# A hybrid attention and state-space layer on one core: the p product moved ahead of the output product, more halves turned through memory, more low parts made by transfer

## The chip, the cores and the metric

The kernel runs on 1 core of one Trainium2 chip. Times are device microseconds of one execution, and the median of several executions stands for a kernel. Besides them there is a profile of one execution: it records when each instruction of each engine ran. PE is the tensor engine (matmuls), PEld its weight loads, DVE the vector engine, ACT the scalar engine, POOL the GpSimd engine, SP the sync engine, which only issues transfers.

## What is computed

One layer on 256 tokens of width 1024, batch 1, everything in float32:

```
h = RMSNorm(x);  [q|k|v|z|xBC|dt|g_a|g_b] = h @ W_in                    # 1024 -> 10272
y_a = attention(q, k, v) @ W_o_attn                                     # 16 heads of 64, causal
y_b = mamba2(z, xBC, dt) @ W_o_ssm                                      # 32 heads of 64, 4 groups, state 128
x = x + (sigmoid(g_a) * y_a + sigmoid(g_b) * y_b) @ W_out
x = x + SwiGLU(RMSNorm(x))                                              # D_FF 2816
x = x + (p @ W_ple_proj) * sigmoid(RMSNorm(x) @ W_ple_gate)             # p: 256 wide
```

With 256 tokens the block attention is plain causal attention, computed in two query tiles of 128.

## The kernel before

**Numbers in three products.** Every operand of a large matmul is split into a rounded high part and a low part (`wh`, `wl` for weights), and a product is made of three matmuls, high by high, high by low and low by high. A weight tile is 128 partitions by 2 x 512 (512 KB). SP loads it into one of 4 buffers `raw`, ACT writes the rounded copy `wh`, DVE subtracts and writes `wl` (`split_w`, line 377). For the tile numbers listed in `BY_DMA` DVE is left out: ACT writes the negated rounded copy into `wl`, and a transfer issued by POOL adds the weights from memory onto it (line 399); then ACT writes `wh`. Tiles are numbered in the order of use from the third panel on, four to a panel of 512 columns.

**Panels.** `PANELS` is the order in which PE goes through the mixers' products: column panels of `W_in` (kinds q, k, v, z, xbc, and the gates ga and gb), then those of `W_o_ssm` (yb, group 0 to 3) and of `W_o_attn` (ya), each for two halves n = 0 and 1 of 512 output columns. A panel of kind xbc is either made by rows, in which the weights are the stationary operand and the result comes out transposed, or by tokens. The list `WIDE` names the xbc and z panels by rows that use the wide form: one matmul of 512 columns, `wh` against both parts of the tokens side by side, and one of 256, `wl` against the high part; ACT copies one half of the result out and DVE adds the other (line 1392). The narrow form has three matmuls of 256 columns, and its result is read where it lies.

**Fillers.** The small work (attention, the scan, the splitting of activations) is written as generators. A counter `fill.now` counts the tensor engine's estimated time, and a generator is taken up when the counter has passed its due time; the tables `LAG` hold those delays, `FLIP` the order inside a few groups of products. A scheduler then sets the order on each engine by rank ("hot", "w", "ev", "bg"), and `follow` adds an order between two instructions.

**Transposes.** They are made in two ways. On PE: a matmul against `ident` (line 297), four of 128x128 for a pair of tiles in `split_pair`. Through memory: DVE transposes blocks of 32 (`turn`, line 739), a transfer writes them to a buffer `turn_d` ("put", lines 749 and 770), and four transfers read them back in the other order ("get", line 759). `MOVED_P` names the pairs of heads whose attention probabilities go through memory (six PE transposes each otherwise). In the class `Sent` the table `VIA` names the engines whose queues issue put and get: p for POOL, s for SP, a for ACT. A name in `FIRST` asks that at most three more low parts (line 377) are made on DVE ahead of the block transposes.

**From the mixers to the feed-forward part.** `joined(n)` makes the gated sum m of half n, and its splitted transpose is the stationary operand of the output product (`pair(m_act, ...)`). That product is made of four pieces: first half of m into result halves n = 0 and 1, then second half of m into n = 0 and 1, 24 matmuls of 512 columns each. `res2.take(n)` adds x, which gives r, and r is split and transposed for the gate and up products. Before the change the first half of m goes through memory and the second is transposed on PE (8 transposes) in the first half of the output product; r's first half goes through memory and its second half is transposed on PE (8 transposes) during the p product (`p @ W_ple_proj`, 24 matmuls), which stands between the output product and the gate product. The gate product begins with r's second half (order of k: 4, 6, 0, 2). After the down product both halves of the next sum, e, go through memory. The p product's result is used only at the very end.

Of the kernel before, what the change touches and what calls it, by code (L numbers as in the profile page):

```python
# [48 lines left out]
    ('k', 1, 1536),  # L49
    ('yb', 0, None),  # L50
    ('z', 2, 4096),
    ('xbc', 3, 6656),
    ('yb', 1, None),
    ('v', 1, 2560),
    ('ga', 1, 8736),
    ('ga', 0, 8224),
    ('yb', 2, 0),
    ('yb', 3, 0),
    ('ya', 0, None),
# [9 lines left out]
def by_rows():  # L69
# [4 lines left out]
WIDE = [('xbc', 0), ('xbc', 2), ('xbc', 3), ('xbc', 4), ('xbc', 5), ('z', 1), ('z', 3)]  # L74
# [15 lines left out]
    "dt": [7695],  # L90
    "dt.t": [1912],
    "dt.e": [44376],
    "dt.low": [0],
    "dt.end": [3600],
    "c.get": [6048, 20580, 4500, 8000, 13800, 5850],
    "z.get": [11120, 4880, 4500, 13235],
    "x.get": [11000, 20471, 9085, 6932],
    "qk.get": [11305, 10811, 11000, 4500],
    "c.moved": [13200, 28401, 10992, 18427, 8500, 31353],
    "c.rows": [0, 1200, 570, 3578, 5000, 1374],  # L100
    "x.moved": [11861, 8500, 57827, 23735],
    "x.start": [4956, 3240, 11800, 11000],
    "x.end": [13264, 5000, 2000, 770],
    "p.moved": [13735, 13200, 13600, 8500, 9650, 8500, 16654, 8500],
    "qk.moved": [10248, 13200, 8500, 8500],
    "qk.split": [0, 3450, 5180, 0],
    "xbc.end": [2853, 15120, 2049, 6195, 16486, 27735],
    "z.turn": [0, 2545, 3366, 0],
    "z.moved": [21550, 8500, 10000, 12100],
    "z.end": [0, 6300, 0, 10600],  # L110
    "qk": [32916, 1650, 4275, 500],
    "qk.turn": [36000, 14411, 4575, 1286],
    "qk.t": [24405, 10000, 1000, 2988, 12758, 5403, 0, 2100],
    "qk.end": [1243, 4652, 5346, 500],
    "v": [500, 8545],
    "cb": [6988, 300, 3282, 0],
    "rows": [32],
    "prep": [590, 750, 3484, 10000, 6191, 5565, 4616, 500],
    "seg": [1326, 0, 2000, 1800, 0, 2818, 0, 810, 0, 0, 4892, 630, 6248, 1305, 0, 0],
    "seg.next": [13744, 2000, 11459, 9286, 0, 13729, 13051],  # L120
    "out": [3000, 14599, 3000, 5070],
    "out.xdt": [300, 10600, 0, 4300],
    "out.end": [0, 1696, 0, 4100],
    "off": [3476, 6856, 3829, 437],
    "off.end": [300, 4316, 925, 2950],
    "finish": [10772, 12064, 10000, 0],
    "finish.ones": [5961, 3915, 3675, 13859],
    "sc": [6504, 10000, 5930, 0, 6130, 2000, 5000, 10000],
    "sc.tr": [2000, 10000, 3000, 13779, 0, 13854, 12691, 0],
    "tr": [0, 14560, 28603, 7222, 8494, 500, 5002, 0],  # L130
    "tr.val": [12661, 0, 3856, 2000],
    "val.end": [7236],
    "m": [11900, 6200],
    "res": [5337, 5987],
    "m.moved": [11625, 22875],
    "r.moved": [15000],
# [53 lines left out]
def tile_layer(ctx: ExitStack, tc: tile.TileContext, head, xk, pt, vec, w_dt, w_big, w_dn2, w_pp, out):  # L190
# [995 lines left out]
    def split_pair(toks, jj, cols, rank="bg"):  # L1186
# [3 lines left out]
        with prio(rank):  # L1190
            pm = pb([2, T])
            for tt in range(2):
                for j in range(2):
                    transpose(pm[:, j, tt * P : tt * P + P], toks[tt][:, (2 * jj + j) * P : (2 * jj + j) * P + P], rank == "hot")
            if cols is None:
                o, ol = both[:, :, 0], both[:, :, 1]
                act(o, pm)
                nc.vector.tensor_sub(ol, pm, o.bitcast(F32))
            else:
                for j in range(2):  # L1200
                    rounded = act(both[:, j, 0], pm[:, j], scale=cols[2 * jj + j])
                for j in range(2):
                    last = stt(both[:, j, 1], pm[:, j], cols[2 * jj + j], both[:, j, 0].bitcast(F32), op0=ALU.mult, op1=ALU.subtract)
                fill.split = last.ins
                fill.rounded = rounded.ins
# [39 lines left out]
    def joined(n, ps=None):  # L1245

        acc, ga = accs[n], gates["ga", n]
        sent = Sent("m") if n == 0 else None
        with prio("ev"):
            for tt in range(2):  # L1250
# [3 lines left out]
                if sent:  # L1254
                    sent.send(tt, acc[:, tt])
        toks = [acc[:, 0], acc[:, 1]]
        if sent:
# [161 lines left out]
    class Residual:  # L1419
# [7 lines left out]
        def take(self, n, pan):  # L1427
            b = self.base[n]
            sent = Sent("r" if self.normed else "e") if self.normed == (n == 0) else None
            with prio("hot"):  # L1430
                for tt in range(2):
                    nc.vector.tensor_add(b[:, tt], pan.ps[tt], b[:, tt])  # L1432
                    if sent:
                        sent.send(tt, b[:, tt])
            if not self.normed:
                if n == 0:
                    fill.spawn(split_moved([b[:, 0], b[:, 1]], self.cols(n), self.acts[n], lag("res") + 20000.0), 0)
                elif sent:
                    fill.spawn(split_moved([b[:, 0], b[:, 1]], self.cols(n), self.acts[n], lag("res"), sent), 0)
                else:  # L1440
                    fill.spawn(split_t([b[:, 0], b[:, 1]], self.cols(n), self.acts[n], lag("res")), 0)
            elif n == 0:
                fill.spawn(split_moved([b[:, 0], b[:, 1]], self.cols(n), self.acts[n], lag_of("r.moved", 0), sent), 0)
# [30 lines left out]
    pair(m_act, res2.take, both=True)  # L1474


    pj = [s4([2, 512]) for _ in range(2)]
    ready = [(1, 0), (1, 1)]
    for n in range(2):
        pan = Panel()  # L1480
        parts = load(w_pp[n], 2)
        for tt, pc in enumerate(pan.pieces):
            for k in range(2):
                pan.step(pc, parts[k], (p_h[:, k], p_l[:, k]), k == 1)
                if 4 * n + 2 * tt + k in SPLITS:
                    res2.split(*ready.pop(0))
        with prio("ev"):
            for tt in range(2):
                copy = nc.vector.tensor_copy(pj[n][:, tt], pan.ps[tt])
                if n == 1:  # L1490

                    follow(copy.ins, fill.split)

# [178 lines left out]
```

## Time and profile before

| what | value |
|---|---|
| median of 3 runs | 574.41 us (574.36 to 575.73) |
| the profiled execution: time | 575.04 us |
| its span, first to last instruction | 573.3 us |
| granted clock of PE | 1.000 |
| PE busy | 567.6 us, 99% |
| PE weight loads | 476.0 us, 83% |
| DVE busy | 443.6 us, 77% |
| ACT busy | 339.2 us, 59% |
| POOL busy | 110.4 us, 19% |
| bytes moved | 124.11 MB, 216 GB/s |

The profiled execution took 0.63 us more than the median, and 1.74 us of its time lie outside the span. Matmuls are pipelined: the mean of one matmul in a group is its duration from start to end, and the next may start long before that end. What a matmul costs PE is the distance from its start to the next start.

### The profile page before, as it was taken

What the parts mean: (1) busy time and instruction counts of PE and PEld (TensorE: products, weight loads), DVE (VectorE), ACT (ScalarE), POOL (GpSimd) and SP (SyncE); (2) the same over time, 40 slices, a digit from 0 to 9 for tenths busy, and PEclk for the clock granted to TensorE, in tenths of its full rate; (3) what the DMA queues carried; (4) which work ended last, traced back from release to release, by engine and by line L of the source; (5) the groups of instructions that cost most, each with busy time, mean ns of one, the idle gap of its engine ahead of it and who ended that gap; (6) DMA issues with size and microseconds to landing.
All of it is one profiled execution on the core that took longest, in us unless ns stands there. A gap on an engine that the chain in (4) does not pass through costs nothing.

```text
span 573.3 us, 8490 instructions
## 1 busy us (share of the span) xinstructions
PE 567.6 (99%) x2971; PEld 476.0 (83%) x2971; DVE 443.6 (77%) x702; ACT 339.2 (59%) x532; POOL 110.4 (19%) x163
## 2 busy tenths in 40 slices
PE   9999999999999999999999999999999999999996
PEld 8887898988888888888887888888888888888885
DVE  6678899989999988898695977766767767646564
ACT  6855567676769578748574444645455455444452
POOL 2011223000532413211320200300312112202020
PEclk9999999999999999999999999999999999999999
DMA  9885698656476756758655786585887887857752
GB/s 314 326 259 179 220 264 234 208 159 181 156 189 183 205 176 174 255 166 252 188 168 186 248 275 225 168 274 183 259 287 228 237 255 246 255 177 254 221 149 74
DMA packets 41179, 124.11 MB, mean 216 GB/s; under 512 B 5424, under 2 KB 10576, under 8 KB 41136
## 3 DMA queue, kind: packets, MB, share of 16 engines
q1 hardware_dynamic: 34432, 104.82, 57.1%
q0 software_dynamic: 6128, 18.09, 12.3%
q10 hardware_dynamic: 576, 0.66, 0.4%
q8 instruction: 23, 0.38, 0.3%
q14 instruction: 20, 0.16, 0.1%
HBM read 114.16 MB, written 9.32 MB: 215 GB/s over the span
## 4 chain that ended last, share of the span: by engine, by line
PE 95%; DVE 2%; DMA 1%; issue 1%; ACT 0%; ACTq 0%
PE g L275 84%; PE pb L275 8%; PE pb L297 2%; DMA raw<-in_w_big 1%; PE pb L309 1%; DVE s L653 1%; DVE wl L377 0%; ACT wh L254 0%; DVE s L660 0%; DVE s L1392 0%; ACT s L254 0%; DVE s L1585 0%; DVE s L1586 0%; DVE tiny_dt L600 0%; DVE tiny_dt L609 0%
## 5 line engine op out<-in xcount | busy, mean ns | idle before, releaser
L275 PE MATMUL g<-wh,s 128*128 128x512 f32 (+1 forms) x1220 | 382.0, 390 | 0.0
L254 ACT ACTIVATE wh<-raw 128x1024 fp32r<-128x1024 f32 (+2 forms) x192 | 198.7, 1039 | 165.1 <-PE g L275 128.9
L377 DVE TENSOR_TENSOR wl<-raw,wh 128x1024 fp32r<-128x1024 f32 (+2 forms) x188 | 223.7, 1194 | 85.4 <-ACT wh L254 83.7
L275 PEld LDWEIGHTS g<-wh,s 128*128 128x128 f32 x1220 | 228.7, 189 | 47.7 <-issue 0.5
L275 PE MATMUL g<-wl,s 128*128 128x512 f32 (+1 forms) x610 | 235.7, 388 | 0.0
L275 PEld LDWEIGHTS g<-wl,s 128*128 128x128 f32 x610 | 114.6, 188 | 23.0 <-issue 0.4
L275 PE MATMUL g<-s,wh 128*128 128x512 f32 (+1 forms) x320 | 90.3, 353 | 0.2 <-DVE s L1392 0.2
L275 PE MATMUL g<-s,wl 128*128 128x256 f32 x256 | 69.2, 283 | 0.0
L275 PEld LDWEIGHTS g<-s,wh 128*128 128x128 f32 x320 | 54.8, 190 | 7.2 <-DVE s L1392 0.6
L275 PEld LDWEIGHTS g<-s,wl 128*128 128x128 f32 x256 | 48.5, 189 | 2.0 <-issue 0.2
L749 POOL DMA_DIRECT2D turn_d<-s x28 | 21.7, 775 | 140.5 <-DVE s L739 140.5
L759 POOL DMA_DIRECT2D s<-turn_d x64 | 35.4, 570 | 57.4 <-DMA turn_d<-s 41.4
L254 ACT ACTIVATE s<-s 128x512 f32<-128x512 f32 (+4 forms) x45 | 34.8, 785 | 16.2 <-DVE s L1432 5.6
L275 PEld LDWEIGHTS pb<-s,s 128*64 128x64 f32 (+2 forms) x336 | 23.9, 158 | 5.8 <-issue 2.4
L275 PE MATMUL pb<-s,s 128*64 128x128 f32 (+5 forms) x336 | 28.7, 294 | 0.0
L254 ACT ACTIVATE s<-pb 128x512 f32<-128x512 f32 (+3 forms) x45 | 20.3, 480 | 13.7 <-PE pb L275 8.4
L254 ACT ACTIVATE s<-s,vecs 128x256 f32<-128x256 f32 (+1 forms) x48 | 23.3, 536 | 5.6 <-DMA s<-turn_d 4.6
L653 DVE SCALAR_TENSOR_TENSOR s<-s,vecs,s 128x255 f32<-128x255 f32 (+2 forms) x60 | 26.5, 480 | 0.0
L886 POOL TENSOR_SCALAR_AFFINE_SELECT rr<-a_h 128x512 fp32r<-128x512 f32 x16 | 16.6, 1094 | 38.7 <-PE pb L275 22.4
L739 DVE STREAM_TRANSPOSE s<-s 128x512 f32<-128x512 f32 (+2 forms) x34 | 22.0, 660 | 1.8 <-ACT s L254 1.5
L254 ACT ACTIVATE s<-s,tiny 128x128 f32<-128x128 f32 (+1 forms) x44 | 18.7, 444 | 5.9 <-DVE tiny L1086 5.9
L794 POOL TENSOR_TENSOR tiny<-tiny,mhalf 128x8 f32<-128x8 f32 x8 | 13.2, 1647 | 42.3 <-DVE tiny L792 42.3
(152 smaller groups left out, 379.9 us busy)
## 6 DMA issues: line engine op xcount, KB each, us to landing
raw<-in_w_big SPq DMA_DIRECT2D x176, 512.0 KB
turn_d<-s POOLq DMA_DIRECT2D x24, 256.0 KB, 5.0
s<-turn_d POOLq DMA_DIRECT2D x48, 128.0 KB, 5.3
wl<-in_w_big POOLq DMA_DIRECT2D x5, 512.0 KB, 8.2
raw<-in_head SPq DMA_DIRECT2D x4, 512.0 KB
s<-in_xk SPq DMA_DIRECT2D x4, 512.0 KB
raw<-in_head SPq DMA_DIRECT2D x6, 256.0 KB
turn_d<-s POOLq DMA_DIRECT2D x6, 192.0 KB, 3.1
```

What stands on the lines that cost most here:

```text
L254: return nc.scalar.activation(o, i, f, **kw)
L275: ins = nc.tensor.matmul(o, lhsT, rhs, start=start, stop=stop).ins
L297: queue(nc.tensor.transpose(o, i, ident[: i.shape[0], : i.shape[0]]).ins, main)
L309: nc.tensor.matmul(pw[:, :P], zero, zero, start=True, stop=True)
L377: low = nc.vector.tensor_sub(wl, raw, wh.bitcast(F32))
L653: stt(cc[j][:, sft:], pu[:, j, : T - sft], cw[j][3 - sft], cc[j][:, sft:], op0=ALU.mult, op1=ALU.add)
L739: turned_by.append(nc.vector.transpose(t_.rearrange("p b (x j) -> p x b j", j=32), src.rearrange(f"p {dims[1]} -> p x b j", b=4, j=32)).ins)
L749: nc.gpsimd.dma_start(d[:, :, at : at + t_.shape[2]].rearrange("b p n -> p b n"), t_)
L759: by[via[b % len(via)]].dma_start(o[32 * b : 32 * b + 32], d[b].rearrange("(a i) n -> i a n", i=32))
L794: nc.gpsimd.tensor_tensor(f, ms, mhalf, op=ALU.pow)
L886: nc.gpsimd.affine_select(r, bcast(a_h[:, c, h0 : h0 + 4].bitcast(F32), P), pattern=[[0, 4], [1, P]], compare_op=ALU.is_ge, fill=0.0, base ...
```

## The change

1. **The p product stands ahead of the output product** and takes its own accumulators (`Panel(aside=True)`); p is loaded and split three panels before the end of `PANELS` (`load_p`).
2. **Both second halves there go through memory**: m's second half (`m1`) and r's second half (`r`), put by SP and read by ACT's queue (`VIA` "s", "a"). r's first half is now the one that PE transposes, inside the last piece of the output product, and the gate product takes k in the order 0, 2, 4, 6.
3. **A fourth pair of probabilities**, (1, 0), goes through memory.
4. **More low parts by transfer**: `BY_DMA` has 11 tiles instead of 5.
5. Panel xbc 1 takes the wide form. `WIDE` loses z 3, which is made by tokens before and after, so that the entry had no effect.
6. z 2 is one place earlier and v 1 two places; of the last panels ya 0 and the first half of yb 3 change places. Nearly all numbers of `LAG` and `FLIP` are new.

```diff
-WIDE = [('xbc', 0), ('xbc', 2), ('xbc', 3), ('xbc', 4), ('xbc', 5), ('z', 1), ('z', 3)]
+WIDE = [('xbc', 0), ('xbc', 1), ('xbc', 2), ('xbc', 3), ('xbc', 4), ('xbc', 5), ('z', 1)]
...
-    ('yb', 3, 0),
-    ('ya', 0, None),
+    ('ya', 0, None),
+    ('yb', 3, 0),
...
-    "res": [5337, 5987],
-    "m.moved": [11625, 22875],
-    "r.moved": [15000],
+    "e.moved": [23750],
+    "r.t": [2062],
+    "m.moved": [19988, 8500],
+    "r.moved": [8500],
...
-MOVED_P = {(1, 1), (1, 2), (1, 3)}
-BY_DMA = {25, 37, 46, 53, 63}
-FIRST = ("e",)
-VIA = {"m": ("p", "p"), "r": ("p", "p"), "e": ("s", "sa")}
-SPLITS = (4, 6)
+MOVED_P = {(1, 0), (1, 1), (1, 2), (1, 3)}
+BY_DMA = {22, 24, 26, 37, 45, 46, 48, 52, 58, 66, 75}
+FIRST = ("m1", "r", "e")
+VIA = {"m0": ("p", "p"), "m1": ("s", "a"), "r": ("s", "a"), "e": ("s", "sa")}
...
-            parts = split_pair(toks, jj, cols)
+            parts = split_pair(toks, jj, cols, "hot")
...
 def joined(n, ps=None):
-        sent = Sent("m") if n == 0 else None
-        with prio("ev"):
+        sent = Sent(f"m{n}")
+        with prio("hot" if n else "ev"):
...
-        if sent:
-            fill.spawn(split_moved(toks, None, m_act[n], lag_of("m.moved", n), sent), 0)
-        else:
-            fill.spawn(split_t(toks, None, m_act[n], lag_of("m", n)), 0)
+        fill.spawn(split_moved([acc[:, 0], acc[:, 1]], None, m_act[n], lag_of("m.moved", n), sent), 0)
...
 def take(self, n, pan):
-            sent = Sent("r" if self.normed else "e") if self.normed == (n == 0) else None
+            sent = Sent("r" if self.normed else "e") if n else None
...
+            if n:
+                fill.spawn(split_moved(rows, self.cols(n), self.acts[n], lag("r.moved" if self.normed else "e.moved"), sent), 0)
+            elif self.normed:
+                fill.hot, fill.ahead = added.ins, 2
+                fill.spawn(split_t(rows, self.cols(n), self.acts[n], lag("r.t")), 0)
+            else:
+                fill.spawn(split_moved(rows, self.cols(n), self.acts[n], 20000.0 + lag("e.t")), 0)
...
-    pair(m_act, res2.take, both=True)
+    p_h, p_l = p_rows
     pj = [s4([2, 512]) for _ in range(2)]
     for n in range(2):
-        pan = Panel()
+        pan = Panel(aside=True)
...
+    pair(m_act, res2.take, both=True)
...
-    for n, k in enumerate((4, 6, 0, 2)):
+    for n, k in enumerate((0, 2, 4, 6)):
```

Line numbers of the changed kernel are higher by one in most of the places named here (275 is 276, 297 is 298, 399 is 400, 759 is 760).

**PE, first half of the output product, second result half.** `g` is the accumulator, s the split tokens, s_454 the gated sum m of the second half. Before, two groups of four transposes stand between its matmuls:

```order
L275 MATMUL g_3718<-wh_3732,s_721_3640 128x512
L275 MATMUL g_3718<-wl_3733,s_721_3640 128x512
L275 MATMUL g_3718<-wh_3732,s_721_3640 128x512
L297 MATMUL pb_3777<-ident,s_454_2368 128x128 x4
L275 MATMUL g_3718<-wh_3732,s_721_3640 128x512
L275 MATMUL g_3718<-wl_3733,s_721_3640 128x512
L275 MATMUL g_3718<-wh_3732,s_721_3640 128x512
L297 MATMUL pb_3788<-ident,s_454_2368 128x128 x4
L275 MATMUL g_3717<-wh_3738,s_722_3648 128x512
```

In the changed kernel the same piece has matmuls alone (they are not shown). The transposes that are left at this boundary stand in the last piece of the output product, on r's first half (s_738):

```order
L276 MATMUL g_3765<-wl_3892,s_772_3820 128x512
L276 MATMUL g_3765<-wh_3891,s_772_3820 128x512
L298 MATMUL pb_3918<-ident,s_738_3694 128x128 x4
L276 MATMUL g_3765<-wh_3891,s_772_3820 128x512
L276 MATMUL g_3765<-wl_3892,s_772_3820 128x512
L276 MATMUL g_3765<-wh_3891,s_772_3820 128x512
L298 MATMUL pb_3931<-ident,s_738_3694 128x128 x4
L276 MATMUL g_3765<-wh_3897,s_773_3828 128x512
```

What moved: the eight transposes of m's second half are gone, and those of r (s_733 in the p product before) stand six matmuls before the end of the output product's last piece.

**ACT, the first half of the output product.** Before, ACT rounds weights, takes m's first half out of what came back from memory (s_721, s_722) and goes on rounding:

```order
L254 ACTIVATE wh_3726<-raw_3725 128x1024
L254 ACTIVATE s_721_3640<-s_704_3545 128x256 x2
L254 ACTIVATE s_722_3648<-s_704_3545 128x256 x2
L254 ACTIVATE wh_3732<-raw_3731 128x1024
L254 ACTIVATE wh_3738<-raw_3737 128x1024
L254 ACTIVATE wh_3808<-raw_3807 128x1024
L254 ACTIVATE wh_3814<-raw_3813 128x1024
```

Now four transfers that read m's second half back (s_750 from `turn_d`) stand in ACT's own order, two and two around a rounding, and the splitting of that half (s_772, s_773) behind them:

```order
L255 ACTIVATE wh_3779<-raw_3778 128x1024
L255 ACTIVATE s_748_3714<-s_712_3540 128x256 x2
L255 ACTIVATE s_749_3722<-s_712_3540 128x256 x2
L255 ACTIVATE wh_3785<-raw_3784 128x1024
L760 DMA s_750_3733<-turn_d_3683 32x4x256 x2
L255 ACTIVATE wh_3849<-raw_3848 128x1024
L760 DMA s_750_3733<-turn_d_3683 32x4x256 x2
L255 ACTIVATE wh_3855<-raw_3854 128x1024
L255 ACTIVATE s_772_3820<-s_750_3733 128x256 x2
L255 ACTIVATE s_773_3828<-s_750_3733 128x256 x2
L255 ACTIVATE wh_3891<-raw_3890 128x1024
```

What moved: ACT issues the reads of the second half and holds what is behind them until the put has landed. The reads of r's second half stand in ACT's order in the same way, two and two around a rounding.

**POOL, during the panels xbc 4 and xbc 0.** The names: `wl` from `in_w_big` is a low part made by transfer, `rr` the decay matrices of the scan that POOL makes from `a_h` once DVE has that, `s` from `turn_d` a get. Before:

```order
L749 DMA turn_d_849<-s_158_847 128x4x128
L759 DMA s_163_885<-turn_d_738 32x4x256 x4
L399 DMA wl_1135<-in_w_big 128x1024
L886 AFFINE_SELECT rr_1363<-a_h 128x512
L886 AFFINE_SELECT rr_1367<-a_h 128x512
L886 AFFINE_SELECT rr_1526<-a_h 128x512
L886 AFFINE_SELECT rr_1530<-a_h 128x512
L759 DMA s_182_1011<-turn_d_849 32x4x256 x4
L399 DMA wl_1658<-in_w_big 128x1024
```

Now:

```order
L750 DMA turn_d_844<-s_159_842 128x4x128
L400 DMA wl_1021<-in_w_big 128x1024
L760 DMA s_161_849<-turn_d_738 32x4x256 x4
L400 DMA wl_1088<-in_w_big 128x1024
L887 AFFINE_SELECT rr_1372<-a_h 128x512
L887 AFFINE_SELECT rr_1376<-a_h 128x512
L887 AFFINE_SELECT rr_1517<-a_h 128x512
L887 AFFINE_SELECT rr_1521<-a_h 128x512
L400 DMA wl_1209<-in_w_big 128x1024
L760 DMA s_182_966<-turn_d_844 32x4x256 x4
L400 DMA wl_1640<-in_w_big 128x1024
```

What moved: there are two more low parts by transfer in this place; the first stands ahead of a get, and the third behind the four `AFFINE_SELECT` that wait for `a_h`, where before the only one stood ahead of them.

More of the change, by code (lines that the diff above doesn't have):

```diff
@@ L89 @@
 LAG = {
-    "dt": [7695],
-    "dt.t": [1912],
-    "dt.e": [44376],
+    "dt": [7225],
+    "dt.t": [1956],
+    "dt.e": [44111],
     "dt.low": [0],
[L94 to L133, printed above, removed]
-    "res": [5337, 5987],
-    "m.moved": [11625, 22875],
-    "r.moved": [15000],
+    "dt.end": [10000],
+    "c.get": [7950, 14964, 4550, 4500, 4500, 4500],
@@ new lines @@
+    "z.get": [9577, 4500, 13420, 29932],
+    "x.get": [11000, 25888, 11280, 10625],
+    "qk.get": [8652, 8013, 4500, 10200],
+    "c.moved": [15000, 46441, 8500, 17726, 8500, 8500],
+    "c.rows": [0, 0, 8304, 3578, 6350, 5000],
+    "x.moved": [8500, 16600, 39658, 34319],
+    "x.start": [7912, 5484, 0, 8550],
+    "x.end": [11424, 4580, 1380, 4500],
+    "p.moved": [13034, 8500, 10000, 10000, 8500, 9432, 8500, 10011],
+    "qk.moved": [12500, 13200, 13625, 8500],
+    "qk.split": [2000, 6620, 4548, 5800],
@@ new lines @@
+    "xbc.end": [16132, 21494, 2049, 4700, 5643, 31757],
+    "z.turn": [0, 1875, 10000, 13450],
+    "z.moved": [8500, 16760, 8500, 10000],
+    "z.end": [13896, 15378, 7000, 13808],
+    "qk": [20905, 4731, 4275, 700],
+    "qk.turn": [36000, 14417, 5000, 114],
+    "qk.t": [26813, 15780, 0, 5913, 12758, 6124, 10000, 2100],
+    "qk.end": [2000, 5548, 1000, 550],
+    "v": [2000, 12000],
+    "cb": [6988, 0, 4840, 0],
+    "rows": [2300],
+    "prep": [0, 0, 3787, 10000, 5144, 5707, 5100, 0],
@@ new lines @@
+    "seg": [2475, 800, 300, 500, 0, 4430, 1537, 0, 0, 2000, 4800, 2800, 14908, 0, 0, 900],
+    "seg.next": [13744, 1475, 0, 9286, 8100, 15709, 9500],
+    "out": [2550, 8439, 19477, 7186],
+    "out.xdt": [2000, 7654, 0, 659],
+    "out.end": [0, 590, 3286, 5195],
+    "off": [9303, 1928, 12500, 0],
+    "off.end": [0, 4316, 0, 4360],
+    "finish": [10772, 4456, 15937, 1038],
+    "finish.ones": [15272, 19395, 1145, 17538],
+    "sc": [7078, 9568, 7756, 4, 4568, 2800, 5858, 1800],
+    "sc.tr": [500, 1625, 27872, 15587, 0, 5787, 20702, 12113],
@@ L137 @@
+    "tr": [300, 10556, 5000, 7222, 5845, 20075, 2934, 0],
+    "tr.val": [850, 5000, 8500, 12209],
+    "val.end": [0],
+    "m": [5000, 11832],
+    "e.t": [3598],
+    "e.moved": [23750],
+    "r.t": [2062],
+    "m.moved": [19988, 8500],
+    "r.moved": [8500],
 }
@@ L1627, in _layout @@
     pairs = [b.reshape(P, 2, 2, 512) for b in blocks[0] + blocks[1][:2]]
-    pairs = [pairs[2 * n + k // 2][:, k % 2] for k in (2, 3, 0, 1) for n in range(3)]
+    pairs = [pairs[2 * n + k // 2][:, k % 2] for k in (0, 1, 2, 3) for n in range(3)]
     blocks[:2] = [[np.concatenate(pairs[k : k + 2], axis=1) for k in range(0, 12, 2)], blocks[1][2:]]
```

71 lines of the change are left out of this document (28 added, 43 removed).

## The prediction

> **What bounds the kernel now.** I read the page first: span, busy shares, chain; then what PE waited for; then PE's timeline at the places that the change touches.
>
> ```profile
> span 573.3 us, 8490 instructions
> PE 567.6 (99%) x2971; PEld 476.0 (83%) x2971; DVE 443.6 (77%) x702; ACT 339.2 (59%) x532; POOL 110.4 (19%) x163
> PE 95%; DVE 2%; DMA 1%; issue 1%; ACT 0%; ACTq 0%
> ```
> ```profile
> PE pb L309 <- PEq L1661: 0.8, 1, 0.8
> PE g L275 <- DVE s L1392: 0.2, 1, 0.2
> ```
>
> PE is the bound: 95% of the chain that ended last is its own work. Of what PE waits for (total, times, longest, in us) one row lies inside the stream, 0.2 us. Two kinds of gain are left: PE work that is not issued, and that wait. All else (more transfers, less DVE work, another order) can only cost: the other engines have room on average, and what counts is whether a result is in time where PE wants it.
>
> **Transposes that go.** The order has 90 transposes against `ident` instead of 104: eight of m's second half, six of the probability pair. Their price is a distance between starts (columns: start, duration, operation). First r's two blocks of before, which have the shape of m's, then a probability pair:
>
> ```profile
> 363.66 0.40 PE L275 MATMUL g<-wh,s 128*128 128x512 f32 x1
> 363.89 0.60 PE L297 MATMUL pb<-ident,s 128*128 128x128 f32 x4
> 364.25 0.47 PE L275 MATMUL g<-wh,s 128*128 128x512 f32 x1
> 364.56 0.39 PE L275 MATMUL g<-wl,s 128*128 128x512 f32 x1
> 364.79 0.63 PE L275 MATMUL g<-wh,s 128*128 128x512 f32 x2
> ...
> 236.22 0.28 PE L275 MATMUL g<-s,wl 128*128 128x256 f32 x1
> 236.34 0.82 PE L297 MATMUL pb<-ident,s 128*128 128x128 f32 x6
> 236.92 0.36 PE L275 MATMUL g<-s,wl 128*128 128x256 f32 x1
> 237.12 0.39 PE L275 MATMUL g<-s,wh 128*128 128x512 f32 x1
> ```
>
> A 512-column matmul follows the last after 0.23 us (363.66 to 363.89). Four transposes take 0.36 (to 364.25), and the matmul behind them 0.31 instead of 0.23: 0.44 us for a block, 0.88 for m's two. The six take 0.58, and the matmul behind 0.20 instead of 0.12 (236.22 to 236.34): 0.66. Together 1.54 us less. The order shows that the remaining transposes are cut into one more group than the three that go would leave: 0.08 back. Net 1.46.
>
> The durations would say another thing:
>
> ```profile
> L297 PE MATMUL pb<-ident,s 128*128 128x128 f32 x104 | 15.6, 272 | 0.0
> ```
>
> By 272 ns each, 14 transposes are 3.8 us. I take the starts, since four transposes lie within 0.36 us; the other price is a rival below. Of the Trainium skill, "TensorE: Matmul & The Clock Gate", section "Part 4: PE-mode transpose", states about 275 ns for a transpose in a kernel's context. The duration agrees, the starts do not; by it the sum below would be some 2.3 us larger.
>
> **xbc 1 in the wide form.** A step of 256 + 256 x 2 becomes 512 + 256, at 32 steps; seven narrow steps lie between the first two rows, six wide ones between the next two:
>
> ```profile
> 82.12 0.28 PE L275 MATMUL g<-s,wl 128*128 128x256 f32 x1
> ...
> 84.64 0.28 PE L275 MATMUL g<-s,wl 128*128 128x256 f32 x1
> 84.76 0.40 PE L275 MATMUL g<-s,wh 128*128 128x512 f32 x1
> ...
> 86.88 0.40 PE L275 MATMUL g<-s,wh 128*128 128x512 f32 x1
> 90.14 0.40 PE L275 MATMUL g<-s,wh 128*128 128x512 f32 x1
> 90.78 0.50 PE L275 MATMUL g<-s,wh 128*128 128x512 f32 x1 [0.24 <-DVE s L1392]
> ```
>
> 2.52/7 = 0.360 against 2.12/6 = 0.353: 32 x 0.007 = 0.22 us less. What it adds is ACT copies and the additions of line 1392, of 0.41 us (row below), and DVE has gaps on average.
>
> The last two rows are the 0.2 us wait: their starts are 0.64 apart where 0.23 is normal, so it cost 0.41. It ended on the addition of another wide panel, which stood behind two convolutions (line 653) that read the accumulators of a narrow one:
>
> ```profile
> 89.43 0.18 DVE L610 CAST a_h<-tiny_dt 128x64 fp32r<-128x64 f32 x1
> 89.53 0.86 DVE L653 SCALAR_TENSOR_TENSOR s<-g,vecs,s 128x254 f32<-128x254 f32 x2
> 90.31 0.41 DVE L1392 TENSOR_TENSOR s<-g,s 128x256 f32<-128x256 f32 x1
> ```
>
> In the new order this row of work is another one; I take 0.4 as gone. From the other side, a like wait can come up elsewhere; I charge 0.3 for that. The ends are 0 and the prices in the rivals.
>
> **m's and r's second halves through memory.** Nearest is e, which takes this way already:
>
> ```profile
> 548.06 0.38 SPq L770 DMA_DIRECT2D turn_d<-s  x1
> 551.37 0.85 ACTq L759 DMA_DIRECT2D s<-turn_d  x2
> 552.34 1.06 ACT L254 ACTIVATE wh<-raw 128x1024 fp32r<-128x1024 f32 x1 [1.92 <-PE g L275]
> 556.28 1.71 ACT L254 ACTIVATE s<-s,vecs 128x256 fp32r<-128x256 f32 x4 [2.88 <-DMA s<-turn_d]
> ...
> 342.69 0.69 DVE L1253 SCALAR_TENSOR_TENSOR s<-s,s 128x512 f32<-128x512 f32 x1
> ...
> L739 DVE STREAM_TRANSPOSE s<-s 128x512 f32<-128x512 f32 x26 | 17.8, 698 | 0.3
> ```
>
> Put to first get is 3.3 us, and get to split 4.9 at most (551.37 to 556.28). With ACT issuing all four, m1 takes: DVE's last addition, two sums and a block transpose, about 2.6 (0.41, as line 1392's, twice 0.69 and 0.70, with gaps), put 3.3, gets, a rounding and gets 0.85 + 1.06 + 0.85, landing 4.9: 13.6, and the first split ends about 14.1 us after the last product of ya 1. PE wants it after the p product (24 matmuls) and two pieces (48): 72 x 0.227 = 16.3 (0.227 is the mean distance of such matmuls; the rows above have 0.23). 2.2 us to spare. r's second half: 13.8 against the gate product's 72 matmuls on the first half, 2.5 to spare. Cost 0. The cover is those 72 matmuls; each us beyond the 2 costs a us. Behind ACT's wait on the put stand roundings of weights, which the order places some 8 us ahead of their use; the wait there was 2.88 us. DVE's block transposes may stand behind one low part (1.22 us in the group of line 377), which the slack holds too.
>
> **r's first half, on PE.** Its transposes stand 15 matmuls (3.4 us) behind the product's end; the addition (0.41) of the last piece and the one ahead of it end at 1.1, or 2.3 behind a low part. Splitting, as before:
>
> ```profile
> 364.53 0.84 ACT L254 ACTIVATE s<-pb,vecs 128x256 fp32r<-128x256 f32 x2 [1.48 <-PE pb L297]
> 365.40 0.88 DVE L1203 SCALAR_TENSOR_TENSOR s<-pb,vecs,s 128x256 fp32r<-128x256 f32 x2 [1.31 <-ACT s L254]
> ```
>
> From 363.89 to 366.28 are 2.4 us: 5.8 against 24 matmuls and a block, 24 x 0.227 + 0.9 = 6.3 when the gate product starts. Only 0.5 to spare; the price is between 0 and 0.7 (one low part in the way). Before, p's product covered this. I take 0, with the 0.3 above as its allowance.
>
> **Low parts by transfer.** Eleven instead of five: six times ACT has 1.06 more, DVE 1.22 less, POOL 0.95 more, and 3.1 MB are moved more. Nothing of it is on PE. The tight place is tiles 22, 24, 26:
>
> ```profile
> 82.37 1.06 ACT L254 ACTIVATE wh<-raw 128x1024 fp32r<-128x1024 f32 x1 [2.18 <-DMA raw<-in_w_big]
> 87.55 1.06 ACT L254 ACTIVATE wl<-raw 128x1024 fp32r<-128x1024 f32 x1 [0.41 <-PE g L275]
> 88.91 0.96 POOL L399 DMA_DIRECT2D wl<-in_w_big  x1 [13.18 <-ACT wl L254]
> 89.69 2.59 POOL L886 TENSOR_SCALAR_AFFINE_SELECT rr<-a_h 128x512 fp32r<-128x512 f32 x4
> 99.59 0.28 PE L275 MATMUL g<-s,wl 128*128 128x256 f32 x1
> ```
> ```profile
> DMA to landing us min/median/max: 7.2/8.2/9.2
> ```
> ```profile
> 71.70:86.00 14.30, 14.30 (x113) 13.95 (x112) 13.48 (x28) 8.86 (x14) 3.67 (x6) 1.00 0.90 264
> 86.00:100.30 14.30, 14.06 (x80) 11.98 (x80) 14.27 (x30) 10.37 (x18) 5.53 (x9) 1.00 0.88 235
> ```
>
> Before's one tile there is issued at 88.91 and lands 9.2 later, at 98.1, 1.4 us ahead of its use at 99.59; the DMA engines are 0.88 to 0.90 busy (second column from the right; then GB/s). The third tile now stands behind the four selects, so not before 89.69 + 2.59 = 92.3; it lands at 99.5 to 101.5, for a use at about 101.7. I take 0; the bound from above is the third rival.
>
> **Sum.** -1.46 - 0.22 - 0.41 + 0.3 = -1.8. The profiled execution took 575.04 (its span 573.3, 1.74 outside), 0.63 over the median of 574.41. So 573.2 for a like execution, and 572.6 for the median. What a measurement tells from no change is 0.3%, 1.7 us: the forecast stands barely beyond it.
>
> **Rivals.**
> 1. Small waits give it back: r's first half late (0 to 0.7), and a landing late by up to a us. About 1 us lost: 573.5, within the bound. For it: 0.5 us of slack; against it: only one wait inside the stream before.
> 2. The other side: the low parts by transfer come late between 79 and 102 us. From the point where a landing takes over about 10.6 us from the rounding's start, or `a_h` (89.43 before) comes over 1 us later, PE waits at each of three tiles; at 1.3 us each that is 3.9, so 576.5. For it: the DMA share of 0.90, ACT waiting 2.18 us for a weight tile, 1 MB more there. Against it: the other landings took 7.2 to 8.2. The Trainium skill, "SBUF — State Buffer", section "SBUF: two separate sides", says that a transfer issued by POOL can starve while DVE holds the port that they share. DVE is 13.5 of 14.3 us busy here; no run here shows that it lengthens a landing.
> 3. Transposes at 272 ns: 3.8 us instead of 1.46, so about 570.3.
>
> **Chances.** Forecast 0.46, own range 571.6 to 573.0, of it 0.06 above 572.69 (574.41 less 0.3%); rival 1 0.25; rival 2 0.16; rival 3 0.05; the rest, 0.08, is a wait at another place of the new order, half of it within the bound and half beyond. Faster: 0.40 + 0.05 = 0.45. Same: 0.06 + 0.25 + 0.04, and 0.01 of rival 2 with one late tile: 0.36. Slower: 0.15 + 0.04 = 0.19. The range reaches from 571.0, between forecast and rival 3, to 576.0, short of three tiles late.
>
> **What the profile after would show.** PE 565.5 to 566 us busy and no row of waits over 0.5 inside the stream. Right on transposes: 90 of line 298, and the first half of the output product with matmuls 0.23 apart throughout. On the second halves: ACT's split of m1 starts 1 to 3 us ahead of PE's use. On r: no gap of PE where the gate product starts. The forecast is wrong if PE's waits name `wl` from memory near 90 to 102 us, or the split of r (line 1201 or so), or if the DMA share there reaches 1.

## The result, and the profile after

| | before | after |
|---|---|---|
| median of 20 executions each | 574.85 us (573.74 to 576.10) | 577.95 us (574.86 to 583.25) |
| ratio, 95% interval | | 1.0052 [1.0033, 1.0071] |
| profiled execution | 575.04 us, span 573.3 | 578.62 us, span 576.9 |
| mean granted clock of PE there | 1.000 | 0.997 |

The change made the kernel about 0.5% slower, where 0.3% faster was forecast, and its executions spread over 8 us instead of 2. The median lies above the forecast's range, which ended at 576.0 us (by the ratio it would be 577.4 beside the 574.41 us that the forecast started from), and the direction was wrong. The page of the changed kernel, the lines that answer to those of before:

```profile
span 576.9 us, 8427 instructions
PE 567.4 (98%) x2925; PEld 472.7 (82%) x2925; DVE 440.1 (76%) x704; ACT 345.3 (60%) x546; POOL 119.3 (21%) x169
PE 86%; DMA 7%; issue 3%; DVE 2%; ACT 1%; POOL 1%; ACTq 0%; SPq 0%; POOLq 0%; DVEq 0%
```

DMA holds 7% of the chain that ended last, 1% before. What PE waited for (total, times, longest):

```profile
PE g L276 <- ACT s L255: 2.0, 1, 2.0
PE g L276 <- DMA wl<-in_w_big: 1.9, 1, 1.9
PE pb L310 <- PEq L1651: 0.8, 1, 0.8
PE g L276 <- DVE wh L374: 0.3, 1, 0.3
```

Two waits of 2 us are new, and before's wait on DVE near 90 us is gone. **The first** is for a low part by transfer (PE, then ACT and POOL; start, duration, operation):

```profile
94.89 0.63 PE L276 MATMUL g<-s,wh 128*128 128x512 f32 x2
97.44 0.39 PE L276 MATMUL g<-s,wl 128*128 128x256 f32 x1 [1.92 <-DMA wl<-in_w_big]
```
```profile
84.44 1.05 ACT L255 ACTIVATE wl<-raw 128x1024 fp32r<-128x1024 f32 x1
85.78 0.93 POOL L400 DMA_DIRECT2D wl<-in_w_big  x1 [3.06 <-ACT wl L255]
88.02 3.76 POOL L887 TENSOR_SCALAR_AFFINE_SELECT rr<-a_h 128x512 fp32r<-128x512 f32 x4 [1.31 <-DVE a_h L611]
91.73 0.87 POOL L400 DMA_DIRECT2D wl<-in_w_big  x1
```
```profile
DMA to landing us min/median/max: 9.3/9.5/11.6
```

It is tile 24, the second of three, issued at 85.78 and landed 11.6 us later (the last row is of the three between 60 and 100 us; before, one tile took 9.2). The third, behind the four selects, was in time. **The second** is r's second half, which ACT reads back and splits (SP, ACT, then PE; the earlier rows of SP and ACT are of m's second half):

```profile
338.13 3.10 SPq L771 DMA_DIRECT2D turn_d<-s  x2
366.48 3.13 SPq L771 DMA_DIRECT2D turn_d<-s  x2
370.37 27.87 SPq L396 DMA_DIRECT2D raw<-in_w_big  x11
```
```profile
345.91 0.82 ACTq L760 DMA_DIRECT2D s<-turn_d  x2
353.98 1.34 ACT L255 ACTIVATE s<-s 128x256 fp32r<-128x256 f32 x4 [5.03 <-DMA s<-turn_d]
372.27 0.79 ACTq L760 DMA_DIRECT2D s<-turn_d  x2
373.20 2.06 ACTq L760 DMA_DIRECT2D s<-turn_d  x2
384.71 1.31 ACT L255 ACTIVATE s<-s,vecs 128x256 fp32r<-128x256 f32 x3 [7.11 <-DMA s<-turn_d]
```
```profile
382.91 0.39 PE L276 MATMUL g<-wh,s 128*128 128x512 f32 x1
385.27 0.50 PE L276 MATMUL g<-wh,s 128*128 128x512 f32 x1 [1.97 <-ACT s L255]
385.61 0.40 PE L276 MATMUL g<-wl,s 128*128 128x512 f32 x1
386.59 0.63 PE L276 MATMUL g<-wl,s 128*128 128x512 f32 x1
387.87 0.63 PE L276 MATMUL g<-wl,s 128*128 128x512 f32 x1
389.72 0.40 PE L276 MATMUL pb<-wh,s 128*128 128x512 f32 x1
```

From the first get to the split 12.4 us pass for r, 8.1 for m's second half. The forecast had 7.7 for both: 2.8 for the gets with a rounding between them, then e's 4.9. Behind this wait the matmuls are slow: from 386.59 to 387.87 are three distances of 0.43 instead of 0.23. The windows say why, in the third column from the right, the granted clock (then DMA share, GB/s):

```profile
345.90:354.00 8.10, 8.10 (x37) 6.70 (x37) 5.47 (x7) 2.11 (x3) 0.00 (x0) 1.00 1.04 267
372.30:384.70 12.40, 11.00 (x49) 8.79 (x47) 2.73 (x3) 2.12 (x2) 1.09 (x3) 1.00 0.96 239
386.00:390.00 4.00, 4.00 (x13) 3.12 (x12) 3.92 (x9) 3.34 (x6) 0.00 (x0) 0.58 0.17 46
```

After the wait the clock was halved for about 3.5 us. And while the gets of m and r were under way, the DMA engines were full. In the kernel before, the same windows for e's gets and for those of r's first half (which landed in 3.4 us):

```profile
551.40:556.30 4.90, 4.90 (x30) 4.33 (x29) 1.51 (x2) 1.08 (x2) 1.07 (x3) 1.00 0.68 161
364.40:370.00 5.60, 5.60 (x28) 4.63 (x28) 3.64 (x7) 4.48 (x8) 3.18 (x7) 1.00 0.40 125
```

The account of the span: I give each matmul the median distance to its follower that its kind (its shape, transposes apart) has in the kernel before, and sum. That is 555.4 us before and 553.5 after, 1.9 less (1.4 less if a kind is the pair of a matmul's shape and its follower's, so the sum is good to half a us); the forecast's terms for PE work make 1.7. Against it stand, in distances, 2.08 at 97 us and 3.88 between 380 and 400 us (2.13 for the wait, 1.75 for the clock), while 0.41 near 90 us are gone. -1.9 + 2.08 + 3.88 - 0.41 = 3.65, beside 3.6 in the spans.

### The profile page after: what moved, and what is told of

Same layout as the page of the kernel before. It is cut to its first block, busy times and chain, and to the rows that moved or that the text cites. A ratio compares the mean times of both kernels' runs of the same rounds, so it can differ in the third digit from the quotient of the medians.

```text
span 576.9 us, 8427 instructions
## 1 busy us (share of the span) xinstructions
PE 567.4 (98%) x2925; PEld 472.7 (82%) x2925; DVE 440.1 (76%) x704; ACT 345.3 (60%) x546; POOL 119.3 (21%) x169
## 4 chain that ended last, share of the span: by engine, by line
PE 86%; DMA 7%; issue 3%; DVE 2%; ACT 1%; POOL 1%; ACTq 0%; SPq 0%; POOLq 0%; DVEq 0%
PE g L276 77%; PE pb L276 7%; DMA s<-turn_d 3%; DMA wl<-in_w_big 2%; PE pb L298 2%; DMA turn_d<-s 1%; ACT wh L255 1%; DVE wl L378 1%; DMA raw<-in_head 1%; DVE s L1435 0%; ACT s L255 0%; DVE s L740 0%; POOL s L760 0%; ACTq L760 0%; POOL turn_d L750 0%
## 5 line engine op out<-in xcount | busy, mean ns | idle before, releaser
L276 PE MATMUL g<-wh,s 128*128 128x512 f32 (+1 forms) x1204 | 377.9, 391 | 2.4 <-ACT s L255 2.0
L378 DVE TENSOR_TENSOR wl<-raw,wh 128x1024 fp32r<-128x1024 f32 (+2 forms) x182 | 216.7, 1196 | 78.1 <-ACT wh L255 77.0
L276 PEld LDWEIGHTS g<-wh,s 128*128 128x128 f32 x1204 | 225.7, 188 | 50.0 <-ACT s L255 2.9
L276 PE MATMUL g<-wl,s 128*128 128x512 f32 (+1 forms) x602 | 233.1, 389 | 0.0
L276 PEld LDWEIGHTS g<-s,wh 128*128 128x128 f32 x288 | 50.4, 188 | 7.5 <-issue 0.2
L255 ACT ACTIVATE s<-s,vecs 128x256 f32<-128x256 f32 (+1 forms) x52 | 25.8, 544 | 12.3 <-DMA s<-turn_d 11.6
L654 DVE SCALAR_TENSOR_TENSOR s<-s,vecs,s 128x255 f32<-128x255 f32 (+2 forms) x72 | 32.3, 488 | 0.7 <-ACT s L255 0.6
L255 ACT ACTIVATE s<-pb 128x512 f32<-128x512 f32 (+3 forms) x41 | 18.6, 474 | 10.6 <-PE pb L276 4.8
L795 POOL TENSOR_TENSOR tiny<-tiny,mhalf 128x8 f32<-128x8 f32 x8 | 16.8, 2100 | 37.3 <-DVE tiny L793 36.9
L740 DVE STREAM_TRANSPOSE s<-s 128x512 f32<-128x512 f32 (+2 forms) x38 | 24.1, 654 | 0.4
L887 POOL TENSOR_SCALAR_AFFINE_SELECT rr<-a_h 128x512 fp32r<-128x512 f32 x16 | 14.8, 943 | 40.3 <-PE pb L276 39.0
```

The source lines that it names most:

```text
L255: return nc.scalar.activation(o, i, f, **kw)
L276: ins = nc.tensor.matmul(o, lhsT, rhs, start=start, stop=stop).ins
L378: low = nc.vector.tensor_sub(wl, raw, wh.bitcast(F32))
L654: stt(cc[j][:, sft:], pu[:, j, : T - sft], cw[j][3 - sft], cc[j][:, sft:], op0=ALU.mult, op1=ALU.add)
L740: turned_by.append(nc.vector.transpose(t_.rearrange("p b (x j) -> p x b j", j=32), src.rearrange(f"p {dims[1]} -> p x b j", b=4, j=32)).ins)
L795: nc.gpsimd.tensor_tensor(f, ms, mhalf, op=ALU.pow)
```

## The experiments

The first theory: two late landings, and the clock behind the second, are the whole loss.

**One place at a time.** no24: `BY_DMA` without 24. r_pool: r by POOL. both: the two together.

```diff
-BY_DMA = {22, 24, 26, 37, 45, 46, 48, 52, 58, 66, 75}
+BY_DMA = {22, 26, 37, 45, 46, 48, 52, 58, 66, 75}
```
```diff
-"r": ("s", "a")
+"r": ("p", "p")
```

> The changed kernel without tile 24 among the low parts by transfer (DVE makes it). Theory (that transfer landed 11.6 us after its issue and PE waited 1.92 us for it): the wait near 97 us goes, tiles 22 and 26 land in 7 to 9 us, and the median falls by 1.9 from 577.95 to about 576.0. Rival (the DMA engines are saturated there, whatever tile is moved): the next tile, 26, comes late instead, a wait of 1 to 2 us stands near 100 us, 577 to 578.

> The changed kernel with the put and the gets of r's second half issued by POOL instead of SP and ACT; PE's order is unchanged. Theory (the way by SP and ACT lands late, 9 to 12 us after the gets' issue, where POOL's gets of r's first half landed in 3.4 us in the kernel before): the wait of 1.97 us near 385 us goes, and with it the 3.5 us after it in which the granted clock was halved (about 1.6 us); 577.95 - 3.6 = 574.4. Rival (the weight loads beside it set the landing, not the queue): the gets land as late, the wait stays within 0.5 us, 577.5 to 578.5.

> Both edits at once. Theory: PE has no wait over 0.5 us inside the stream, clock 1.000, and the gains that were forecast show: 577.95 - 1.9 - 3.6 = 572.4, about 0.4% faster than the kernel before. Rival (the transposes and the wide form save less than the 1.7 us that the starts give, or a third cost sits elsewhere): 574 to 575, no difference to the kernel before.

Measured: 577.65 (ratio 1.0039 [1.0021, 1.0057]), 582.06 (1.0116 [1.0098, 1.0135]) and 580.73 (1.0097 [1.0077, 1.0116]). In no24 PE waited 0.7 us for tile 26 instead, and r's wait was still 1.8: nearer to its rival. r_pool refutes that the queue was at fault; there the wait grew, since both trips were slow (POOL, ACT, PE of r_pool):

```profile
371.73 0.81 POOL L771 DMA_DIRECT2D turn_d<-s  x1
379.03 2.25 POOL L760 DMA_DIRECT2D s<-turn_d  x4 [5.30 <-DMA turn_d<-s]
```
```profile
388.01 1.71 ACT L255 ACTIVATE s<-s,vecs 128x256 fp32r<-128x256 f32 x4 [6.44 <-DMA s<-turn_d]
```
```profile
388.57 0.80 PE L276 MATMUL g<-wh,s 128*128 128x512 f32 x1 [5.38 <-ACT s L255]
```

The put took 7.3 us (371.73 to the get at 379.03) and the gets 9. The DMA share was 0.90 and 0.89 during the two trips. So the landing of 3.4 us that POOL's gets had in the kernel before belonged to a quiet place, not to POOL. In both, with no wait at 97 us, r's wait was 4.2 us.

**The price of a transpose.** Each issued twice, in the kernel before:

```diff
 def transpose(o, i, main=False):
-        queue(nc.tensor.transpose(...).ins, main)
+        for _ in range(2):
+            queue(nc.tensor.transpose(...).ins, main)
```

> The kernel before with each of its 105 PE transposes issued twice. Priced by distances between starts (0.09 to 0.11 us each): +9.5 to +11.5 us, about 585. Priced by their duration of 0.272 us: +28.6 us, about 603. Waits elsewhere may add to both; the distances between starts in its profile decide.

Measured 587.52, 12.5 us more for 105 transposes: 0.119 us each, with no wait added:

```profile
L298 PE MATMUL pb<-ident,s x208: 270/272/328, 58.6 to 378.6; 128*128 128x128 f32 x104
```

The duration is 272 ns still; the price is near that of the starts. So the forecast's price of a transpose was near right, and its third rival is out.

**What makes r late, and whether m does.** r_held holds the load of weight tile 113, and so all loads behind it on SP, until r's gets have landed (a copy of one column from them, which the load overwrites). r_pe transposes r's second half on PE. r_pe_low does so too and takes 22, 24, 26 out of `BY_DMA`. m_pe transposes m's second half on PE.

```diff
 def load_tiles(src, nk):
+                if tile_no[0] in HELD:                    # {113}
+                    nc.gpsimd.tensor_copy(tiles[0][:, 0, 0:1], held["r"][:, 0, 0:1])
                 nc.sync.dma_start(tiles[0], src[:, k : k + 2])
```
```diff
 def take(self, n, pan):                                   # r_pe
-            sent = Sent("r" if self.normed else "e") if n else None
+            sent = Sent("e") if n and not self.normed else None
...
-            if n:
+            if n and not self.normed:
```

> The changed kernel, in which the load of weight tile 113 (first used at about 388 us) and all loads behind it wait for the gets of r's second half. Theory (the weight loads that are queued beside put and gets set their landing): the gets land 4 to 6 us after their issue instead of 9 to 12, PE's wait near 385 us and the halved clock behind it go, 577.95 - 3.6 = 574.3, if the held tiles still come in time. Rival (the gets' own small packets, or ACT that issues them late, set the landing): it stays at 9 to 12 us, and with the held loads the time is 578 or more.

> The changed kernel with r's second half transposed on PE too (8 more transposes, in the gate product); put and gets of r are gone. Theory: the wait of 2 us near 385 us and the halved clock (1.6) go, the transposes cost 0.9 (by starts) to 0.95 (by 0.119 us each, the kernel with doubled transposes): about 575.3, and the spread of the runs, 8 us, shrinks to that of the other late landing. Rival (the time is lost at many places and this wait only passes it on): 577 to 579.

> The same, and tiles 22, 24 and 26 get their low parts from DVE. Theory: no wait over 0.5 us is left, 575.3 - 1.9 = 573.4, 0.3% faster than the kernel before, spread under 3 us. Rival: the work that DVE takes back there (3 x 1.22 us) or waits elsewhere keep it at 575.

> The changed kernel with m's second half transposed on PE, r's second half through memory as in the change. Theory (ACT's wait for m's gets and their traffic push the weight loads back, which then meet r's put and gets): r's gets land sooner, 6 to 8 us, the wait near 385 us falls below 1 us, and with 0.9 for the transposes the median is 576 to 577. Rival (r's gets meet loads that are there anyway): the wait stays at 2 us, 578.8.

Measured: 576.63 (1.0027 [1.0009, 1.0045]), 576.53 (1.0030 [1.0008, 1.0052]), 581.81 (1.0119 [1.0098, 1.0141]), 577.48 (1.0040 [1.0025, 1.0054]). r_held decides between the theories on r:

```profile
375.15 1.28 ACTq L765 DMA_DIRECT2D s<-turn_d  x3
381.24 1.71 ACT L256 ACTIVATE s<-s,vecs 128x256 fp32r<-128x256 f32 x4 [3.63 <-DMA s<-turn_d]
```
```profile
375.10:381.20 6.10, 6.10 (x29) 5.05 (x28) 1.71 (x2) 1.06 (x1) 1.28 (x3) 1.00 0.67 172
```

The same gets by the same queue took 6.1 us instead of 12.4, at a DMA share of 0.67 instead of 0.96, and PE no longer waited there. So the weight loads beside the gets set their landing. The median is 1.3 below the change's only: the profiled execution has the wait at 97 us (1.8), now with the halved clock behind it, and 0.5 on m's second half. r_pe removed the wait as well and paid for its transposes; it was left with 2.5 us at 97 us. m_pe left r's wait at 0.3 in its profile, with 2.6 at 97 us and 1.0 on m's first half. But its theory is not borne out: r's gets still took 11.5 us from the first get to the split, not 6 to 8. They went out 0.8 us sooner after the start of the gate product (4.7 us instead of 5.5) and took 0.9 us less. r_pe_low refutes my cure for that place: without the three transfers PE waits elsewhere,

```profile
120.86 0.92 PE L276 MATMUL pb<-s,s 128*128 128x256 f32 x4 [2.22 <-DVE s L661]
```

for DVE, which has their three low parts back. DVE falls behind: POOL's four selects, which wait for DVE's `a_h`, start at 94.24 instead of 88.02. Just ahead of the wait DVE itself stood 2.4 us for a rounding by ACT whose weights came late; that the one caused the other is not shown.

**The place near 97 us.** All four have r held. hold27 and hold28 hold the load of tile 27, or 28, until tile 24 has landed; hold3 is hold28 with tile 103 held behind m's gets; tile25 puts 25 in place of 22, 24, 26 in `BY_DMA`.

```diff
-HELD = {113: 'r'}
+HELD = {27: 24, 113: 'r'}               # hold27
+HELD = {28: 24, 113: 'r'}               # hold28
+HELD = {28: 24, 103: 'm1', 113: 'r'}    # hold3
```

> The changed kernel with tile 113 held behind r's gets (576.63 alone) and, besides, the load of weight tile 27 and what SP issues behind it held until the low part of tile 24 has landed. Theory (the transfers by POOL land late near 90 us since weight loads share the DMA engines with them): tile 24 lands in 9.5 us or less instead of 11.6 to 12.3, PE's wait near 97 us falls below 0.3, 576.6 - 1.9 - some of the halved clock = 574.2, if tile 27 still comes in time (used near 104 us). Rival (POOL's own queue, with eight gets and three low parts in it, sets the landing): 11 us or more, the wait stays, 576.6 or more.

> The same with tile 28 held instead of 27, PE's order unchanged: one weight load more shares the engines. Theory: tile 24 lands about 1 us earlier than in the change, the wait near 97 us is 0.5 to 1.5, about 575.3; later tiles are in no danger. Rival: as without it, 576.6.

> As with tile 28, and besides tile 103 held behind m1's gets. Theory: m1's gets land 2 us earlier than the 7 to 8 us after their issue, the wait of up to 0.5 us on them goes, 0.3 less than with tile 28 alone: 575.0. Rival: the held load makes a wait of its own near 360 us, 576 or more.

> The changed kernel with tile 113 held behind r's gets, and tile 25 (as in the kernel before) made by transfer in place of 22, 24 and 26. Theory: one such transfer lands in 9 us as it did before, no wait near 97 us, 576.6 - 1.9 = 574.7. Rival (DVE needs what the three transfers take off it here, as the run without any of the three showed, which waited 2.2 us on DVE near 121 us): 577 or more.

Measured: 579.88 (1.0075 [1.0055, 1.0095]), 576.80 (1.0029 [1.0018, 1.0041]), 578.30 (1.0050 [1.0032, 1.0067]; one execution of 3243.5 us is a stray) and 578.41 (1.0064 [1.0044, 1.0084]). In none does PE wait at 97 us. In hold28 the slowest of the transfers up to 130 us took 9.6 us instead of 11.6, 2 us less where its theory had 1. But waits come up behind it:

```profile
107.71 0.55 PE L277 MATMUL g<-s,wh 128*128 128x512 f32 x1 [1.93 <-ACT wh L256]
```
```profile
107.49 0.50 PE L277 MATMUL g<-s,wh 128*128 128x256 f32 x2 [0.43 <-ACT wh L256]
108.75 0.39 PE L277 MATMUL g<-s,wl 128*128 128x256 f32 x1 [0.76 <-DVE wl L379]
122.98 1.70 PE L277 MATMUL pb<-s,s 128*128 128x256 f32 x14 [0.57 <-ACT e L256]
```

The first row is of hold27, the others of hold28. The first three are weights that came late because loads were held; the last is a small product's wait for ACT, which r_pe_low and tile25 have too, with 0.6 us. The engines for transfers were at 1.05 there in the change (94 to 98 us, 308 GB/s), so that holding one passed the wait on to another. hold3's profile is of its fastest execution, 575.58; it has waits of 0.8 us near 108 and 118 us and of 0.3 at 357 us, where tile 103 was held. tile25 has no wait over 0.6 in its profile (576.58), and yet a median of 578.41; where its slower executions lose time is not on record.

**Halves of the change.** front_only takes the changed tables up to the output product with before's code from there; back_only the reverse. back_held, back_r_pe and back_2held are back_only with r's load held, with r on PE, and with both m's and r's loads held (103 and 113).

In short form, the tables that each takes over:

```diff
 front_only, against the kernel before
+PANELS, WIDE, MOVED_P, BY_DMA, FLIP and LAG (but for m, res, r and e) of the changed kernel
 back_only, against the changed kernel
+PANELS, WIDE, MOVED_P, BY_DMA, FLIP and LAG (but for m, r and e) of the kernel before
```

> The changed kernel's tables for all that lies ahead of the output product (panels, the wide form, pairs of probabilities, low parts by transfer, delays), with the kernel before's code from there on (m's second half and r's second half on PE, the p product between). Theory (two separate costs): PE work is 0.66 + 0.22 - 0.08 less, the wait near 97 us adds 2 and in some executions the halved clock 1.6: 575.4 to 576.5, spread of 5 us or more. Rival (all of it comes from the back): 574.2, spread under 3 us.

> The reverse: the kernel before up to the output product, the change from there on (p product ahead, both second halves through memory). Theory: 0.88 less PE work, the wait near 385 us adds 2 and mostly the halved clock 1.6: 576 to 577.5. Rival (the weight loads at the back are late only because the front fell behind): r's gets land in time, 574.0.

> The same with the load of weight tile 113 held behind r's gets. Theory: no wait near 385 us, no low parts late near 97 us: 574.9 - 0.9 = 574.0, spread under 3 us, 0.15% faster than the kernel before. Rival: m1's gets or the held loads cost what it saves, 574.9 or more.

> The kernel before up to the output product, then the change with r's second half transposed on PE: only m's second half is saved. Theory: 574.9 - 0.9 = 574.0, spread as before, below 2.5 us. Rival: m1's put and gets make the weight loads late elsewhere, 574.9 or more.

> The kernel before up to the output product, the change from there on, with tile 103 held behind m1's gets and tile 113 behind r's. Theory (landings under weight loads are all that is wrong at the back): m1's gets land within 5 us, no wait near 355 and 385 us, the 0.88 of the transposes is left over: 574.0, spread below 3 us. Rival (the jitter of the landings or the held loads still make waits): 575.5 to 577 with a spread of 5 us, as with r's alone (576.71).

Measured: 582.86 (1.0131 [1.0098, 1.0165]), 577.28 (1.0038 [1.0016, 1.0059]), 576.71 (1.0027 [1.0006, 1.0048]), 579.04 (1.0056 [1.0033, 1.0079]), 578.85 (1.0060 [1.0040, 1.0079]). back_only alone costs as much as the whole change, within the intervals. But the wait is another one; PE in back_only, then ACT and PE in back_2held:

```profile
355.14 0.50 PE L276 MATMUL g<-wh,s 128*128 128x512 f32 x1 [2.00 <-ACT s L255]
385.98 0.50 PE L276 MATMUL g<-wh,s 128*128 128x512 f32 x1 [0.79 <-ACT s L255]
```
```profile
356.69 4.09 ACT L256 ACTIVATE wh<-raw 128x1024 fp32r<-128x1024 f32 x4 [3.05 <-DMA raw<-in_w_big]
357.80 0.50 PE L277 MATMUL g<-wh,s 128*128 128x512 f32 x1 [2.66 <-ACT wh L256]
```

It is m's second half that was late here by 2.0 us, in back_r_pe by 3.2, in back_held by 0.9. In back_2held it comes in time, and the held weights late. None of the orders that were tried fits both: the trip needs its share of the DMA engines just where the weights need nearly all of them. Over all these profiles, the stretch from the first get to the split took 6.1 to 7.5 us where the DMA share was 0.58 to 0.67 (r in r_held, back_held and back_2held, m in back_2held), and 8.1 to 12.4 us where it was 0.93 to 1.04 (both halves in the change and in back_only, r in m_pe, m in r_held and back_held). Within the second group the share does not order them: 8.1 us at 1.04, 12.4 at 0.96. front_only shows the wait on a low part again (3.2 us at 100 us), and a new one of 4.3 us at 348 us on m's first half, which before's code reads by POOL; so it is no measure of the front alone, and how the loss divides between front and back stays open.

**The smallest part alone.** pair10 is the kernel before with the pair (1, 0) of probabilities through memory.

```diff
-MOVED_P = {(1, 1), (1, 2), (1, 3)}
+MOVED_P = {(1, 0), (1, 1), (1, 2), (1, 3)}
```

> The kernel before with the pair (1, 0) of probabilities through memory as the only edit. Theory: 0.66 us of PE work less and no new wait, 574.9 - 0.7 = 574.2. Rival (its put and gets meet the weight loads like the others): 575 to 577.

Measured 575.63 beside 575.34 (1.0007 [0.9998, 1.0016]): no difference, and no new wait over 0.3 us. Its trace has six transposes less (0.40 us less on them between 217 and 293 us), but PE goes between the small products and the weight matmuls 34 times in that stretch instead of 30, and the stretch took 75.3 us as against 75.1. The gain seems to have gone into those changes of form; that is read off the two traces and was not tried.

No kernel here beat the kernel before. So the first theory is not borne out as a whole: both waits are real, but taking one away brought back at most about half of the loss (ratios of 1.0027 in r_held and 1.0030 in r_pe instead of 1.0052, with intervals that overlap), and no run took both away without new waits.

## Why the prediction was wrong

- **PE work.** Right in mechanism and size: 90 transposes, the output product free of them, 0.119 us each in the doubling where the starts gave 0.09 to 0.11 with the matmul behind; 1.4 to 1.9 us less by distances where 1.7 was forecast. But the one part tried alone, pair10, did not show its 0.7 in the time. The wait at 90 us went, as credited (0.41).
- **r's first half on PE.** Right that it costs nothing: the gate product starts near 366.8 in step, and the first low part, which DVE has done at about the same time, is wanted 0.5 us later. The second pair's split ends only near 368.6, but PE wants that 36 matmuls after the start.
- **"Cost 0" for m's and r's second halves.** This step failed. Its landing, 4.9 us, came from e, at a DMA share of 0.68; at m and r it is 1.04 and 0.96. With the issues ahead of it the forecast had 7.7 us from the first get to the split. r's second half took 12.4, which is 4.7 more; the cover of 72 matmuls (about 366.8 to 383.1) and the slack of 2.5 were worked out rightly, and PE lost the rest, 2.1. m's took 8.1, only 0.4 more, but from its second put (340.85) to the first get passed 5.1 us, at a share of 1.07, where 3.3 was forecast, so that of 2.2 us of slack about 0.4 was left. The rows are the start of the output product and its 48th and 49th matmul, and the 49th, at 354.8, is the first on m's second half:

```profile
343.90 0.39 PE L276 MATMUL g<-wh,s 128*128 128x512 f32 x1
354.56 0.62 PE L276 MATMUL g<-wh,s 128*128 128x512 f32 x2
```

  The first of the four splittings that begin at 353.98 was done near 354.4. In back_only the slack did not hold: 10.8 us to the split, and a wait of 2.0. The kernel before has shares of 0.58 to 0.82 between 346 and 362 us and of 0.80 to 0.88 between 374 and 386 us; the put and gets come on top of these, which I did not work out.
- **The low parts.** These too were put at 0, and cost 2.08. The second rival (which the paragraph on the low parts calls the third) named the place, and put the point at 10.6 us from the rounding's start: tile 24 was rounded at 84.44, landed at 97.4, 13 us later. It charged three tiles, and that paragraph held the third, behind the selects, to be the tight one; it was the second, and one tile alone. With a DMA share of 0.90 ahead of the change its chance of 0.16 looks too low now. With a weight load held, the slowest landing was 9.6 us instead of 11.6 (hold28), which speaks for the loads beside it as the cause. No run separates that from the rule cited there, of the Trainium skill, "SBUF — State Buffer", section "SBUF: two separate sides", by which a transfer issued by POOL can starve while DVE holds the port that they share.
- **The clock** was in no term. It is near half of what the second place cost (1.75 of 3.88).
- **The spread.** The executions of the changed kernel go from 574.86 to 583.25. Only one trace of each kernel is kept, so that landings vary from one execution to the next, and the waits with them, is the likely reason and not shown. The mean granted clock is on record for each: it is 0.997 or less in ten of the 20, with a median of 578.9 us, and 0.998 or more in the others, with 576.0. The kernel before was never below 0.998 in the 109 executions measured beside the experiments. A stretch of 3.4 us at half clock takes 0.003 off the mean, so about half of the changed kernel's executions probably went through one or more. I took one profiled execution's slack as if it were all.

## What to carry to other kernels

Price a transfer by the DMA share of the place where it will run, not by the same transfer in a quiet one, and ask for more slack than the difference between the two. Work taken from the bound engine and given to transfers is free only while the stage has transfer time to spare; where the share was near 1.0 here, holding one transfer back mostly moved the wait to the next. And a wait of the tensor engine of about 2 us can cost twice its length.

## What the runs showed of the hardware

A wait of PE of about 2 us can halve its granted clock for some 3.5 us. It is not the length alone that decides (windows of m_pe after a wait of 2.57 us at 98.6, then of r_pe after 2.47 at 98.7):

```profile
100.00:104.00 4.00, 4.00 (x16) 3.42 (x15) 3.23 (x7) 1.73 (x4) 0.00 (x0) 0.57 1.05 283
```
```profile
100.00:104.00 4.00, 4.00 (x26) 3.48 (x25) 4.00 (x8) 1.48 (x3) 0.00 (x0) 1.00 1.05 283
```

The matmuls started in these 4 us are 16 and 26. Waits of 1.77 (no24), 1.83 (r_held), 1.97 (the change), 2.00 (back_only) and 2.57 us were followed by it, those of 1.68 (r_pool, at 97 us), 1.92 (the change, at 97 us) and 2.47 not. After 4.2 and 5.4 us (both, r_pool) it lasted about 7, but in front_only it lasted about 3.5 after a wait of 4.3 us (a clock of 0.57 from 348 to 352 us, then 1.00) and about 7 after one of 3.2 (0.50 from 100 to 104 us, then 0.77 to 108). The Trainium skill, "TensorE: Matmul & The Clock Gate", section "What's actually happening", has the clock fall after at least one idle window of about 3.4 us, in windows that run freely. The length of the slow stretch and its dependence on more than the gap agree with these runs; that a whole idle window is needed does not, since 1.77 us were enough.
